# A GLA and ConvFFN layer: row squares from row tiles in the head, and three edits at the seam to the up-projection

## The chip, the cores and the metric

The kernel runs on one core of a Trainium2 chip. The metric is the device time of one execution in microseconds (us). TensorE (PE) does the matrix products, VectorE (DVE), ScalarE (ACT) and GpSimd (POOL) the elementwise work, and SyncE (SP) issues most transfers; POOL issues some.

## The reference

One layer (DEPTH is 1) of a decoder trunk, for 1024 tokens of width 1024, all in float32:

```python
x = x + gla_mixer(rms_norm(x, norm1), ...)   # 4 heads, dk 128, dv 256, chunked linear attention
x = x + conv_ffn(rms_norm(x, norm2), ...)    # below, FFN_DIM 2816
return rms_norm(x, final_norm)

def conv_ffn(x, w_up, conv_w, conv_b, w_down):
    u = x @ w_up
    u_pad = jnp.pad(u, ((0, 0), (CONV_WIDTH - 1, 0), (0, 0)))
    u = sum(u_pad[:, j:j + s] * conv_w[j] for j in range(CONV_WIDTH)) + conv_b
    gate, up = jnp.split(u, 2, axis=-1)
    return (jax.nn.silu(gate) * up) @ w_down
```

`rms_norm` multiplies each token's row by `rsqrt(mean(x*x) + 1e-6)` and a gain.

## The kernel before

**Number format.** Every operand of a product is split into two parts: a high part (a cast to the matrix format `F32R`, by ACT) and a low part, the difference (by DVE). `mm3` and `prod` add up three products: high by high, high by low, low by high. `unit(i)` loads a weight block of 128 x 1024 floats (512 KB) into a `raw` tile, of which there are four (`RAW`), and splits it into `whi` and `wlo`. For the blocks in `POOL_SPLIT` the low part is POOL's work; of these the kernel calls `unit` for four, the two plain feature tiles' gate and up weights.

**The head** (0 to about 54 us). The input comes transposed, as eight tiles `xT[kt]` of 128 features by 1024 tokens. Each is multiplied by the norm's gain and split into the big tile `T`; TensorE multiplies it with the q and k weights of head 0 (`q_ps`, `k_ps`), in a loop over `kt`. The norm's scale, one number per token, is applied behind the products. For it ACT squares each xT tile (`sq`), and POOL (the last two: DVE) adds the squares to `sqsum`; eight small products with a column of ones sum over the features (`st_ps`, line 281), giving `ss_1`, and `rsqrt` on POOL makes `rstd_1` of it. `va_mm(tok)` multiplies a tile of 128 tokens with the V weights of head 0; three of these run, then a product of `diag` (the scales on a diagonal, made by DVE) spreads the scales over the partitions (`b_ps`, `rstd_bc`), then `va_mm(3)`. In this stage the order on PE, ACT and DVE is partly as written (`manual_schedule`) and partly a scheduler's; SP's queue runs in order, and a load waits there for its buffer.

**The middle** (54 to about 420 us): linear attention by heads, the gate products, the output projection.

**The seam** (about 420 to 510 us). While the second half of the output projection runs over eight token tiles, `norm2` normalizes each and `feat` transposes it (`t_ps`, in PSUM) into `T`. For tokens 4 to 7 `combine` makes sums and differences of the four quarters of the features and tokens: POOL adds high and low parts back together (`r11`, `r21`), DVE forms `t1` and `t2` from these and from the transposes in PSUM, then the new `r11` and `r21`; all are split into `T` and `T2`, and `r21` goes to memory (`f4_dram`) and comes back as `t4`. The up-projection of the feature tiles 0 and 1 is done plainly (`plain_mm`): first with the first half of the tokens, between the last two `feat`, then with the second half, in PSUM banks that `feat`'s transposes leave. From feature tile 2 on, fewer products are formed with those sums (`xb`, `zb`, `yb`), and POOL adds up the weights (`w_prep`: `s12`, `s34`).

`plain_evac` copies the products to SBUF tiles `y` (four buffers, which the later `yg` and `yu` share); `plain_end` runs the convolution of width 3 along the tokens (`conv`: one ACT instruction, two DVE passes) in tiles `cv` (three buffers), and `gate` does Silu, the product, and the differences that the down-projection uses. From tile 2 on, the convolutions accumulate in PSUM (`ca`); the two plain ones do so in `cv`, in SBUF.

**The rest** (to the end): the up-projection to feature tile 21, the down-projection, the last norm.

Of the kernel before, what the change touches and what calls it, by code (L numbers as in the profile page):

```python
# [14 lines left out]
P = 128  # L15
# [17 lines left out]
RAW = 4  # L33
Y_POOL = (1, 3, 5)
Y_DVE = (6,)
SQ_HP = 5
Q1_A = 2
Q1_B = 3
HALF = 512
# [4 lines left out]
U_O = U_R + 8  # L44
U_F = U_O + 8
N_UNITS = U_F + 3 * NF

POOL_SPLIT = {U_F, U_F + 1, U_F + 2, U_F + 3, U_F + 4, U_F + 5}

V_N1 = 0  # L50
V_BA = V_N1 + KT
# [6 lines left out]
def gla_convffn_kernel(  # L58
# [22 lines left out]
    def load_unit(i):  # L81
        raw = wp.tile([P, 1024], F32, name="raw", tag="raw", bufs=RAW)
        nc.sync.dma_start(out=raw, in_=w[i])
        return raw

    def split_unit(raw, eng):
        hi = wp.tile([P, 1024], F32R, name="whi", tag="whi", bufs=5)
        lo = wp.tile([P, 1024], F32R, name="wlo", tag="wlo", bufs=5)
        nc.scalar.copy(out=hi, in_=raw)  # L89
        eng.tensor_tensor(out=lo, in0=raw, in1=hi.bitcast(F32), op=ALU.subtract)  # L90
        return hi, lo

    def unit(i):
        return split_unit(load_unit(i), nc.gpsimd if i in POOL_SPLIT else nc.vector)

    def mm3(outs, ah, al, bh, bl, start, stop):
        n = len(outs)
# [56 lines left out]
    ast = g1.tile([P, S], F32R, name="ast")  # L154
    ust = g1.tile([P, 4 * P], F32R, name="ust")

    sqsum = g1.tile([P, S], F32, name="sqsum", tag="tmp1")

    def tmp2():
        return g1.tile([P, S], F32, name="tmp2", tag="tmp2")  # L160

# [5 lines left out]
    for kt in range(KT):  # L167
# [35 lines left out]
        if kt == 1:  # L203
            for j in range(2):
                nc.scalar.copy(out=wh[j][:, 256:], in_=wr[j][:, 256:])
                nc.vector.tensor_tensor(out=wl[j][:, 256:], in0=wr[j][:, 256:],
                                        in1=wh[j][:, 256:].bitcast(F32), op=ALU.subtract)
        with tc.high_priority() if kt >= SQ_HP else nullcontext():
            if kt == 0:
                nc.scalar.activation(out=sqsum, in_=raw, func=AF.Square)  # L210
            else:
                sq = g1.tile([P, S], F32, name="sq", tag="tmp2" if kt % 2 else "q_f")
                nc.scalar.activation(out=sq, in_=raw, func=AF.Square)
                eng = nc.gpsimd if kt < KT - 2 else nc.vector
                eng.tensor_tensor(out=sqsum, in0=sqsum, in1=sq, op=ALU.add)
        for ps, whi, wlo in ((q_ps, wh[0], wl[0]), (k_ps, wh[1], wl[1])):
            ks = slice(kt * P, kt * P + P)
            for ns in ([[0], [1]] if kt == 0 else [[0, 1]]):
# [57 lines left out]
    ss_1 = const.tile([P, NG], F32, name="ss_1")  # L276
    ET = mybir.EngineType
    with tc.manual_schedule(engines={ET.PE, ET.Activation, ET.DVE}):
        st_ps = sm.tile([P, NG], F32, name="st_ps", tag="sm")
        for j in range(NG):  # L280
            nc.tensor.matmul(out=st_ps[:, j:j + 1], lhsT=sqsum[:, j * P:(j + 1) * P], rhs=ones[:, 0:1],
                             start=True, stop=True)
        nc.scalar.copy(out=ss_1, in_=st_ps)
        rsqrt(rstd_1, ss_1, D)
        va_ps = [va_mm(tok) for tok in range(3)]
        rhl = [const.tile([P, NG], F32R, name=f"rhl{i}") for i in range(2)]
        nc.vector.tensor_copy(out=rhl[0], in_=rstd_1)
        nc.vector.tensor_tensor(out=rhl[1], in0=rstd_1, in1=rhl[0].bitcast(F32), op=ALU.subtract)
        diag = [g1.tile([P, S], F32R, name=f"diag{i}", tag=f"tmp{i + 1}") for i in range(2)]
        va_evac(0, va_ps[0])  # L290
        for dg, r in zip(diag, rhl):
            nc.vector.tensor_tensor(out=dg.rearrange("p (j t) -> p j t", t=P),
                                    in0=ident.unsqueeze(1).broadcast_to([P, NG, P]),
                                    in1=r.bitcast(F32).unsqueeze(2).broadcast_to([P, NG, P]), op=ALU.mult)
        for n in range(2):
            b_ps = sm.tile([P, HALF], F32, name="b_ps", tag="sm")
            for i in range(2):
                nc.tensor.matmul(out=b_ps, lhsT=ones_r, rhs=diag[i][:, n * HALF:(n + 1) * HALF],
                                 start=i == 0, stop=i == 1)
            nc.scalar.copy(out=rstd_bc[:, n * HALF:(n + 1) * HALF], in_=b_ps)  # L300
            if n == 0:
                va_evac(1, va_ps[1])
        va_ps.append(va_mm(3))
        q_f, k_f = evac_qk(q_ps, k_ps)
# [302 lines left out]
    def combine(t, tb):  # L607
        cs = slice(t * P, (t + 1) * P)
        b12, b22 = tb
        r11, r21, t1, t2 = (rp.tile([P, 4, P], F32, name=n, tag=n) for n in ("r11", "r21", "t1", "t2"))  # L610
        pool_add(r11, T[:, 4, :, cs].bitcast(F32), T[:, 5, :, cs].bitcast(F32))
        pool_add(r21, T[:, 6, :, cs].bitcast(F32), T[:, 7, :, cs].bitcast(F32))
        nc.vector.tensor_tensor(out=t1, in0=r11, in1=b12, op=ALU.subtract)
# [85 lines left out]
    def cv_tile(name):  # L699
        return up.tile([P, S], F32, name=name, tag="cv", bufs=3)  # L700
# [43 lines left out]
        return ys  # L744

    def plain_end(f, ys):
        c = [conv(f, j, ys[j]) for j in range(2)]
        gate(f, c[0], c[1], c[0])

    def w_load(f):  # L750
        return [load_unit(U_F + 3 * f + j) for j in range(2)] if f < NF else None
# [42 lines left out]
            down_mm(bx[t], g, t, i == 0, i == NP2 - 1)  # L794

    with tc.manual_schedule(engines={ET.PE}):
        plain_end(0, plain_evac(0))
        y_last = plain_evac(NPLAIN - 1)

        def finish_products(st):  # L800
            f, xb, zb, wf, yg, yu = st
# [20 lines left out]
        pB_stack.close()  # L822
        pC_stack = ExitStack()
        pC = pC_stack.enter_context(tc.tile_pool(name="pC", bufs=1, space=PSUM, reuse_waits="tile"))
        prev, wn = None, w_load(NPLAIN)
        for f in range(NPLAIN, NF + 1):
            p4, q3 = finish_products(prev) if prev else (
                lambda: None, lambda: plain_end(NPLAIN - 1, y_last))
            if f == NF:
                break  # L830
            if f == NP2:
# [275 lines left out]
```

## Time and profile before

| what | value |
| --- | --- |
| device time, median of 3 runs | 1091.33 us (1090.83 to 1092.58) |
| the profiled execution's own time | 1091.58 us |
| its span in the profile | 1089.8 us |
| TensorE busy | 1068.9 us, 98% |
| DVE, ACT, POOL busy | 730.6, 507.7, 328.9 us |
| mean granted TensorE clock | 0.992 |
| moved by DMA | 149.07 MB, mean 137 GB/s |

The span reaches from the first to the last recorded instruction; the execution's own time is 1.78 us longer. Busy times are of single engines, and overlap. The granted clock is a share of 2.4 GHz: 1.00 is that, 0.50 is 1.2 GHz.

### The profile page before, as it was taken

The page shows a single profiled execution, that of the slowest core. Times are in us where ns is not written, and L with a number is a line of the kernel's source. Part 1 is how long each engine was busy: PE and PEld are TensorE (multiplying, and loading weights), DVE is VectorE, ACT ScalarE, POOL GpSimd, SP SyncE. Part 2 cuts the span into 40 slices and gives each one's busy share as a digit, 9 for nine tenths or more (in the row PEclk, how much of TensorE's full clock was granted, in tenths as well). Part 3 has the DMA queues.
Part 4 walks back from the last instruction along what each step waited for, and adds up shares of the span by engine and source line. Part 5 has one row for each costly group of instructions (what it writes and reads, how often), then busy time and mean ns, then how long its engine had stood idle before and what let it go on. Part 6 is the DMA issues. An engine that isn't in the chain of part 4 may idle for free.

```text
span 1089.8 us, 14045 instructions
## 1 busy us (share of the span) xinstructions
PE 1068.9 (98%) x5288; PEld 905.3 (83%) x5288; DVE 730.6 (67%) x888; ACT 507.7 (47%) x779; POOL 328.9 (30%) x273
## 2 busy tenths in 40 slices
PE   7999999999999999898999999999999999999997
PEld 5889999898888888787888888888888888888885
DVE  7757767575534146867767677677767767997863
ACT  6444636364323035364545455445444545544453
POOL 5100100030631022537443423554645431200311
PEclk8999999999999999999999999999999999999999
DMA  5511111140523131135343434544554469976472
GB/s 203 184 40 59 58 68 50 67 174 32 190 81 126 49 106 39 39 122 197 135 156 116 155 127 155 153 106 126 159 140 108 126 169 329 379 245 198 157 258 90
DMA packets 62996, 149.07 MB, mean 137 GB/s; under 512 B 7120, under 2 KB 9936, under 8 KB 62416
## 3 DMA queue, kind: packets, MB, share of 16 engines
q1 hardware_dynamic: 54240, 125.89, 33.8%
q0 software_dynamic: 8688, 22.29, 8.6%
q8 instruction: 41, 0.67, 0.2%
q14 instruction: 27, 0.22, 0.1%
HBM read 102.80 MB, written 45.35 MB: 136 GB/s over the span
## 4 chain that ended last, share of the span: by engine, by line
PE 91%; DVE 3%; DMA 2%; POOL 2%; ACT 1%; issue 1%; SPq 0%; POOLq 0%; ACTq 0%; DVEq 0%
PE xb L574 20%; PE zb L574 10%; PE bw L776 8%; PE bx L776 5%; PE yb L574 5%; PE o_ps L99 3%; PE o_ps L103 3%; PE o_ps L101 3%; PE bz L776 3%; PE by L776 3%; PE r_ps L99 3%; PE r_ps L103 3%; PE r_ps L101 3%; PE v_ps L103 2%; PE v_ps L99 2%; PE v_ps L101 2%
## 5 line engine op out<-in xcount | busy, mean ns | idle before, releaser
L574 PE MATMUL xb<-T,whi 128*128 128x512 f32 x640 | 198.4, 391 | 3.0 <-ACT yg L841 3.0
L574 PEld LDWEIGHTS xb<-T,whi 128*128 128x128 f32 x640 | 120.8, 189 | 28.5 <-ACT yg L841 3.4
L574 PE MATMUL xb<-T,wlo 128*128 128x512 f32 x320 | 125.0, 391 | 0.0
L548 DVE TENSOR_TENSOR wlo<-s,whi 128x1024 fp32r<-128x1024 f32 x40 | 67.2, 1680 | 54.0 <-ACT whi L547 54.0
L566 POOL TENSOR_TENSOR s<-raw 128x512 f32<-128x512 f32 x40 | 60.4, 1512 | 128.2 <-DVE wlo L548 83.4
L574 PE MATMUL zb<-T,whi 128*128 128x512 f32 x320 | 98.5, 389 | 0.0
L574 PEld LDWEIGHTS xb<-T,wlo 128*128 128x128 f32 x320 | 60.5, 189 | 12.6
L574 PEld LDWEIGHTS zb<-T,whi 128*128 128x128 f32 x320 | 60.1, 188 | 12.5
L566 POOL TENSOR_TENSOR cv<-cv 128x512 f32<-128x512 f32 x14 | 33.2, 2371 | 113.7 <-DVE cv L722 108.4
L481 POOL DMA_DIRECT2D o_dram<-o_sb x16 | 12.0, 749 | 178.1 <-DVE o_sb L476 121.4
L566 POOL TENSOR_TENSOR s<-s,raw 128x512 f32<-128x512 f32 x40 | 64.3, 1607 | 1.6
L548 DVE TENSOR_TENSOR wlo<-raw,whi 128x1024 fp32r<-128x1024 f32 (+1 forms) x40 | 42.2, 1054 | 33.3 <-ACT whi L547 33.3
L574 PE MATMUL zb<-T,wlo 128*128 128x512 f32 x160 | 62.2, 389 | 0.0
L89 ACT CAST whi<-raw 128x1024 fp32r<-128x1024 f32 x32 | 33.6, 1051 | 51.4 <-PE o_ps L103 34.3
L547 ACT CAST whi<-s 128x1024 fp32r<-128x1024 f32 x40 | 42.0, 1050 | 32.6 <-PE xb L574 25.9
L547 ACT CAST whi<-raw 128x1024 fp32r<-128x1024 f32 (+1 forms) x40 | 33.3, 834 | 47.6 <-PE zb L574 29.8
L99 PE MATMUL v_ps<-whi,T 128*128 128x256 f32 x192 | 54.5, 284 | 0.0
L103 PE MATMUL v_ps<-whi,T 128*128 128x256 f32 x192 | 54.5, 284 | 0.0
L101 PE MATMUL v_ps<-wlo,T 128*128 128x256 f32 x192 | 54.4, 283 | 0.0
L776 PE MATMUL bw<-whi 128*128 128x512 f32 x132 | 51.5, 390 | 0.0
L776 PE MATMUL bw<-whi,wlo 128*128 128x512 f32 x132 | 51.4, 389 | 0.0
L776 PE MATMUL bw<-wlo,whi 128*128 128x512 f32 x132 | 51.3, 389 | 0.0
(291 smaller groups left out, 2971.3 us busy)
## 6 DMA issues: line engine op xcount, KB each, us to landing
raw<-in_w_dram SPq DMA_DIRECT2D x74, 512.0 KB, 3.6
t_dram<-cv SPq DMA_DIRECT2D x44, 256.0 KB, 2.6
t_dram<-cv POOLq DMA_DIRECT2D x33, 256.0 KB, 6.7
t<-in_w_dram SPq DMA_DIRECT2D x33, 256.0 KB, 4.0
t<-t_dram SPq DMA_DIRECT2D x33, 256.0 KB, 4.2
ab<-in_w_dram SPq DMA_DIRECT2D x32, 256.0 KB, 3.5
h_dram<-cv SPq DMA_DIRECT2D x14, 512.0 KB, 4.2
ab<-h_dram SPq DMA_DIRECT2D x21, 256.0 KB, 3.0
```

The source lines that it names most:

```text
L89: nc.scalar.copy(out=hi, in_=raw)
L99: nc.tensor.matmul(out=outs[j], lhsT=ah, rhs=bh[j], start=start, stop=False)
L101: nc.tensor.matmul(out=outs[j], lhsT=ah, rhs=bl[j], start=False, stop=False)
L103: nc.tensor.matmul(out=outs[j], lhsT=al, rhs=bh[j], start=False, stop=stop)
L481: nc.gpsimd.dma_start(out=o_dram[:, g - 1:g + 1, h * DV:(h + 1) * DV], in_=o_sb)
L547: nc.scalar.copy(out=dst_hi, in_=src)
L548: nc.vector.tensor_tensor(out=dst_lo, in0=src, in1=dst_hi.bitcast(F32), op=ALU.subtract)
L566: nc.gpsimd.tensor_tensor(out=out, in0=a, in1=b, op=op)
L574: nc.tensor.matmul(out=out, lhsT=a[:, ks], rhs=b[:, kt, :], start=start and kt == 0 and j == 0, stop=kt == 3 and j == 2, skip_group_check= ...
L776: nc.tensor.matmul(out=out, lhsT=a[:, ts], rhs=b[:, H1], start=start and j == 0, stop=stop and j == 2, skip_group_check=True)
```

## The change

1. In the head the squares of the xT tiles and `st_ps` go. Instead SP loads the input a second time, as eight tiles `xr` of 128 tokens by 1024 features (`xt`), and ACT squares each with the row sum (`accum_out`) going straight to a column of `ss_1`.
2. `POOL_SPLIT` goes: the low parts of the four plain weight blocks are DVE's.
3. `r11` and `r21` of `combine` get two buffers each.
4. All plain products are evacuated first. The plain convolutions run behind the closing of `pB`, in PSUM tiles of `pC` that share the tag `c0`; the up half comes first, its second pass goes to a `cv` tile, and the gated product to a tile `h`.

```diff
--- before.py
+++ after.py
@@ -33,7 +33,6 @@
 RAW = 4
 Y_POOL = (1, 3, 5)
 Y_DVE = (6,)
-SQ_HP = 5
 Q1_A = 2
 Q1_B = 3
 HALF = 512
@@ -44,8 +43,6 @@
 U_O = U_R + 8
 U_F = U_O + 8
 N_UNITS = U_F + 3 * NF
-
-POOL_SPLIT = {U_F, U_F + 1, U_F + 2, U_F + 3, U_F + 4, U_F + 5}
 
 V_N1 = 0
 V_BA = V_N1 + KT
@@ -91,7 +88,7 @@
         return hi, lo
 
     def unit(i):
-        return split_unit(load_unit(i), nc.gpsimd if i in POOL_SPLIT else nc.vector)
+        return split_unit(load_unit(i), nc.vector)
 
     def mm3(outs, ah, al, bh, bl, start, stop):
         n = len(outs)
@@ -153,8 +150,6 @@
     rstd_bc = g1.tile([P, S], F32, name="rstd_bc")
     ast = g1.tile([P, S], F32R, name="ast")
     ust = g1.tile([P, 4 * P], F32R, name="ust")
-
-    sqsum = g1.tile([P, S], F32, name="sqsum", tag="tmp1")
 
     def tmp2():
         return g1.tile([P, S], F32, name="tmp2", tag="tmp2")
@@ -205,14 +200,6 @@
                 nc.scalar.copy(out=wh[j][:, 256:], in_=wr[j][:, 256:])
                 nc.vector.tensor_tensor(out=wl[j][:, 256:], in0=wr[j][:, 256:],
                                         in1=wh[j][:, 256:].bitcast(F32), op=ALU.subtract)
-        with tc.high_priority() if kt >= SQ_HP else nullcontext():
-            if kt == 0:
-                nc.scalar.activation(out=sqsum, in_=raw, func=AF.Square)
-            else:
-                sq = g1.tile([P, S], F32, name="sq", tag="tmp2" if kt % 2 else "q_f")
-                nc.scalar.activation(out=sq, in_=raw, func=AF.Square)
-                eng = nc.gpsimd if kt < KT - 2 else nc.vector
-                eng.tensor_tensor(out=sqsum, in0=sqsum, in1=sq, op=ALU.add)
         for ps, whi, wlo in ((q_ps, wh[0], wl[0]), (k_ps, wh[1], wl[1])):
             ks = slice(kt * P, kt * P + P)
             for ns in ([[0], [1]] if kt == 0 else [[0, 1]]):
@@ -276,11 +263,10 @@
     ss_1 = const.tile([P, NG], F32, name="ss_1")
     ET = mybir.EngineType
     with tc.manual_schedule(engines={ET.PE, ET.Activation, ET.DVE}):
-        st_ps = sm.tile([P, NG], F32, name="st_ps", tag="sm")
         for j in range(NG):
-            nc.tensor.matmul(out=st_ps[:, j:j + 1], lhsT=sqsum[:, j * P:(j + 1) * P], rhs=ones[:, 0:1],
-                             start=True, stop=True)
-        nc.scalar.copy(out=ss_1, in_=st_ps)
+            xr = g1.tile([P, D], F32, name="xr", tag=("tmp1", "tmp2", "q_f", "k_f")[j % 4])
+            nc.sync.dma_start(out=xr, in_=xt[j * P:(j + 1) * P, :])
+            nc.scalar.activation(out=xr, in_=xr, func=AF.Square, accum_out=ss_1[:, j:j + 1])
         rsqrt(rstd_1, ss_1, D)
         va_ps = [va_mm(tok) for tok in range(3)]
         rhl = [const.tile([P, NG], F32R, name=f"rhl{i}") for i in range(2)]
@@ -607,7 +593,8 @@
     def combine(t, tb):
         cs = slice(t * P, (t + 1) * P)
         b12, b22 = tb
-        r11, r21, t1, t2 = (rp.tile([P, 4, P], F32, name=n, tag=n) for n in ("r11", "r21", "t1", "t2"))
+        r11, r21, t1, t2 = (rp.tile([P, 4, P], F32, name=n, tag=n, bufs=2 if n[0] == "r" else 1)
+                            for n in ("r11", "r21", "t1", "t2"))
         pool_add(r11, T[:, 4, :, cs].bitcast(F32), T[:, 5, :, cs].bitcast(F32))
         pool_add(r21, T[:, 6, :, cs].bitcast(F32), T[:, 7, :, cs].bitcast(F32))
         nc.vector.tensor_tensor(out=t1, in0=r11, in1=b12, op=ALU.subtract)
@@ -744,8 +731,8 @@
         return ys
 
     def plain_end(f, ys):
-        c = [conv(f, j, ys[j]) for j in range(2)]
-        gate(f, c[0], c[1], c[0])
+        cu = conv(f, 1, ys[1], pC.tile([P, S], F32, name="ca", tag="c0"))
+        gate(f, conv(f, 0, ys[0], pC.tile([P, S], F32, name="ca", tag="c0")), cu, cv_tile("h"))
 
     def w_load(f):
         return [load_unit(U_F + 3 * f + j) for j in range(2)] if f < NF else None
@@ -794,8 +781,7 @@
             down_mm(bx[t], g, t, i == 0, i == NP2 - 1)
 
     with tc.manual_schedule(engines={ET.PE}):
-        plain_end(0, plain_evac(0))
-        y_last = plain_evac(NPLAIN - 1)
+        ys = [plain_evac(f) for f in range(NPLAIN)]
 
         def finish_products(st):
             f, xb, zb, wf, yg, yu = st
@@ -822,10 +808,12 @@
         pB_stack.close()
         pC_stack = ExitStack()
         pC = pC_stack.enter_context(tc.tile_pool(name="pC", bufs=1, space=PSUM, reuse_waits="tile"))
+        if NPLAIN > 1:
+            plain_end(0, ys[0])
         prev, wn = None, w_load(NPLAIN)
         for f in range(NPLAIN, NF + 1):
             p4, q3 = finish_products(prev) if prev else (
-                lambda: None, lambda: plain_end(NPLAIN - 1, y_last))
+                lambda: None, lambda: plain_end(NPLAIN - 1, ys[-1]))
             if f == NF:
                 break
             if f == NP2:
```

SP's queue in the head, before, from xT tile 3 on (`raw_199`; `raw_218` to `raw_275` are xT tiles 4 to 7, `raw_299` and `raw_304` the V weights):

```order
L186 DMA raw_199<-in_xT_dram 128x1024
L223 DMA ident_69<-in_cst_dram 128x128
L225 DMA war_295<-in_wa_dram 128x128
L240 DMA vec_sb_68<-in_vec_dram 128x188
L241 DMA mask_70<-in_cst_dram 128x128
L186 DMA raw_218<-in_xT_dram 128x1024
L186 DMA raw_237<-in_xT_dram 128x1024
L186 DMA raw_256<-in_xT_dram 128x1024
L186 DMA raw_275<-in_xT_dram 128x1024
L83 DMA raw_299<-in_w_dram 128x1024
L83 DMA raw_304<-in_w_dram 128x1024
```

The same place now, from the third row tile on (two more `xr` stand right ahead; `raw_207`, `raw_223`, `raw_239` and `raw_255` are xT tiles 4 to 7, `raw_276` and `raw_281` the V weights):

```order
L268 DMA xr_298<-in_xt_dram 128x1024
L181 DMA raw_207<-in_xT_dram 128x1024
L181 DMA raw_223<-in_xT_dram 128x1024
L181 DMA raw_239<-in_xT_dram 128x1024
L268 DMA xr_301<-in_xt_dram 128x1024
L181 DMA raw_255<-in_xT_dram 128x1024
L268 DMA xr_304<-in_xt_dram 128x1024
L268 DMA xr_307<-in_xt_dram 128x1024
L268 DMA xr_310<-in_xt_dram 128x1024
L80 DMA raw_276<-in_w_dram 128x1024
L80 DMA raw_281<-in_w_dram 128x1024
L268 DMA xr_313<-in_xt_dram 128x1024
```

Three row tiles now stand ahead of xT tile 4, one ahead of tile 7, three ahead of the V weights and one behind them.

ACT's queue in the seam, before, around the copy of the first `yg` (`y_4401` and `y_4404` are the second plain tile's products, `xb_4437` the first sums' product):

```order
L547 CAST T_66<-t4_4360 128x1024
L547 CAST T_66<-t4_4364 128x1024
L727 ACTIVATE cv_4388<-cv_4384 128x512
L547 CAST whi_4528<-raw_4496 128x1024
L742 COPY y_4404<-u_ps_4335 128x512
L711 ACTIVATE cv_4470<-y_4404,vec_sb_68 128x1024
L841 COPY yg_4439<-xb_4437 128x512
L721 ACTIVATE cv_4466<-cv_4466 128x1024
```

And now (`y_4372` and `y_4369` are the first plain tile's, up and gate; `y_4378` the second's up):

```order
L533 CAST whi_4525<-raw_4493 128x1024
L729 COPY y_4378<-u_ps_4326 128x512
L698 ACTIVATE ca_4385<-y_4372,vec_sb_68 128x1024
L704 COPY cv_4386<-ca_4385 128x2
L829 COPY yg_4433<-xb_4431 128x512
L698 ACTIVATE ca_4391<-y_4369,vec_sb_68 128x1024
L533 CAST whi_4533<-s12_4529 128x1024
L834 COPY yg_4433<-xb_4431 128x512
```

Ahead of the copy of `yg` there was the second plain tile's last convolution; now the first plain tile's first one stands there, with its two-column copy.

DVE's queue in the seam, before, from the first plain convolution on:

```order
L712 SCALAR_TENSOR_TENSOR cv_4384<-y_4378,vec_sb_68,cv_4384 128x1023
L548 TENSOR_TENSOR wlo_4416<-raw_4411,whi_4415 128x1024
L714 SCALAR_TENSOR_TENSOR cv_4384<-y_4378,vec_sb_68,cv_4384 128x1022
L712 SCALAR_TENSOR_TENSOR cv_4388<-y_4381,vec_sb_68,cv_4388 128x1023
L548 TENSOR_TENSOR wlo_4424<-s12_4419,whi_4423 128x1024
L714 SCALAR_TENSOR_TENSOR cv_4388<-y_4381,vec_sb_68,cv_4388 128x1022
L548 TENSOR_TENSOR wlo_4430<-s34_4420,whi_4429 128x1024
L548 TENSOR_TENSOR wlo_4434<-raw_4413,whi_4433 128x512
L722 TENSOR_TENSOR cv_4384<-cv_4384,cv_4388 128x1024
L712 SCALAR_TENSOR_TENSOR cv_4466<-y_4401,vec_sb_68,cv_4466 128x1023
L548 TENSOR_TENSOR T_66<-t4_4360,T_66 128x1024
```

And now, from the first weight split of the up-projection on:

```order
L534 TENSOR_TENSOR wlo_4410<-raw_4405,whi_4409 128x1024
L534 TENSOR_TENSOR wlo_4418<-s12_4413,whi_4417 128x1024
L534 TENSOR_TENSOR wlo_4424<-s34_4414,whi_4423 128x1024
L534 TENSOR_TENSOR wlo_4428<-raw_4407,whi_4427 128x512
L534 TENSOR_TENSOR T_66<-t4_4351,T_66 128x1024
L534 TENSOR_TENSOR T_66<-t4_4355,T_66 128x1024
L534 TENSOR_TENSOR wlo_4526<-raw_4493,whi_4525 128x1024
L699 SCALAR_TENSOR_TENSOR ca_4385<-y_4372,vec_sb_68,ca_4385 128x1023
L701 SCALAR_TENSOR_TENSOR cv_4386<-y_4372,vec_sb_68,ca_4385 128x1022
L699 SCALAR_TENSOR_TENSOR ca_4391<-y_4369,vec_sb_68,ca_4391 128x1023
L701 SCALAR_TENSOR_TENSOR ca_4391<-y_4369,vec_sb_68,ca_4391 128x1022
```

The passes of the first plain tile stood between the splits of feature tile 2's weights; now all splits up to the first of feature tile 3 come before them.

## Rows read from the trace of the kernel before

**Rows 1.** The page, part 1: busy us, share of span, instructions of TensorE.
```profile
PE 1068.9 (98%) x5288; PEld 905.3 (83%) x5288; DVE 730.6 (67%) x888; ACT 507.7 (47%) x779; POOL 328.9 (30%) x273
```

**Rows 2.** Waits of TensorE, whole span: us in total, times, longest.
```profile
PE q_ps L101 <- DVE T L197: 5.0, 2, 3.9
PE u_ps L574 <- DVE t L614: 3.6, 1, 3.6
PE xb L574 <- ACT yg L841: 3.0, 1, 3.0
```

**Rows 3.** Timeline of the head: start us, us, engine, what; idle before, releaser.
```profile
13.80 0.73 PE L99 MATMUL q_ps<-T,whi 128*128 128x512 f32 x2
...
14.85 12.21 POOL L215 TENSOR_TENSOR sqsum<-sqsum,sq 128x1024 f32<-128x1024 f32 x4 [0.98 <-ACT sq L213]
...
18.91 1.22 PE L101 MATMUL q_ps<-T,whi 128*128 128x512 f32 x2 [3.91 <-DVE T L197]
...
32.90 0.61 PE L99 MATMUL q_ps<-T,whi 128*128 128x512 f32 x2
...
38.34 1.84 PE L281 MATMUL st_ps<-ones,sqsum 128*128 128x1 f32 x16
...
41.53 0.16 ACT L283 COPY ss<-st_ps 128x8 f32<-128x8 f32 x1
...
44.67 2.35 DVE L292 TENSOR_TENSOR diag<-ident,rhl 128x1024 fp32r<-128x1024 f32 x2
...
50.40 0.40 PE L266 MATMUL va_ps<-T 128*128 128x288 f32 x1 [0.21 <-ACT rstd_bc L300]
```

**Rows 4.** Windows of the head: busy by engine, TensorE clock, DMA share, GB/s.
```profile
0.00:9.00 9.00, 7.23 (x23) 5.72 (x24) 2.67 (x6) 4.07 (x6) 0.71 (x8) 1.00 0.65 201
9.00:12.00 3.00, 3.00 (x11) 2.36 (x11) 1.28 (x2) 2.86 (x4) 0.68 (x1) 1.00 1.03 417
12.00:15.00 3.00, 3.00 (x13) 1.92 (x11) 3.00 (x2) 3.00 (x4) 2.02 (x2) 1.00 0.88 299
36.00:39.00 3.00, 3.00 (x19) 2.57 (x17) 2.01 (x3) 1.74 (x2) 0.00 (x0) 1.00 0.97 365
```

**Rows 5.** ACT, a Square with row sum: ns min/median/max, first and last start.
```profile
L601 ACT ACTIVATE junk<-x2a x4: 1041/1044/1047, 394.1 to 411.4; 128x1024 bf16<-128x1024 f32 x4
L601 ACT ACTIVATION_READ_ACCUMULATOR junk<-x2a x4: 187/190/194, 395.0 to 412.4; 128x1 f32 x4
```

**Rows 6.** Timeline of the seam, first stall.
```profile
453.22 1.03 PE L629 MATMUL t_ps<-ident,x2b 128*128 128x128 f32 x8
...
454.61 2.69 POOL L566 TENSOR_TENSOR r<-T 128x512 f32<-128x512 f32 x2 [6.20 <-DVE T L548]
...
460.33 1.28 DVE L632 TENSOR_TENSOR T<-t_ps,T 128x512 fp32r<-128x512 f32 x2
...
463.35 0.70 PE L574 MATMUL u_ps<-T,whi 128*128 128x512 f32 x2 [3.64 <-DVE t L614]
...
474.55 1.05 ACT L547 CAST whi<-raw 128x1024 fp32r<-128x1024 f32 x1 [1.99 <-DMA raw<-in_w_dram]
```

**Rows 7.** Timeline of the seam, second stall.
```profile
489.15 4.44 POOL L566 TENSOR_TENSOR cv<-cv 128x512 f32<-128x512 f32 x1 [5.29 <-ACT T L547]
...
493.63 1.24 ACT L711 ACTIVATE cv<-y,vec_sb 128x1024 f32<-128x1024 f32 x1 [2.53 <-POOL cv L566]
...
495.39 1.22 PE L574 MATMUL xb<-T,whi 128*128 128x512 f32 x2 [2.97 <-ACT yg L841]
```

**Rows 8.** Windows behind the two stalls of the seam.
```profile
464.00:468.00 4.00, 4.00 (x13) 3.13 (x12) 2.26 (x4) 1.40 (x3) 0.00 (x0) 0.57 0.24 66
495.00:499.00 4.00, 3.61 (x9) 2.90 (x10) 4.00 (x2) 1.29 (x2) 4.00 (x3) 0.57 1.02 335
```

**Rows 9.** DVE convolution passes, on PSUM (ca) and on SBUF (cv): ns min/median/max.
```profile
L712 DVE SCALAR_TENSOR_TENSOR ca<-yu,ncw,ca x8: 1287/1289/1289, 513.0 to 646.3; 128x1023 f32<-128x1023 f32 x8
...
L712 DVE SCALAR_TENSOR_TENSOR cv<-y,vec_sb,cv x4: 1277/1286/2295, 472.6 to 496.8; 128x1023 f32<-128x1023 f32 x4
```

## The prediction

> **What bounds the kernel now.** The page's engine table comes first: TensorE is busy for 98% of the span [rows 1]. Time can then only be won where TensorE waits or runs at a lower clock, so the list of its waits is next. It has three long entries [rows 2]: 5.0 us in the head (a T low half from DVE), 3.6 us and 3.0 us in the seam. None of the others is above 1.0 us, and none lies between 54 and 450 us or behind 500 us. The change touches just these two places; of the instructions behind them only names and line numbers differ.
>
> In the head, the timeline [rows 3] shows TensorE at contraction tile 2 (13.80 us), then idle until 18.91 us, because DVE's low halves are slow while POOL adds squares (four adds, 12.21 us, from 14.85 us). The adds end in eight small products `st_ps` that keep TensorE for 1.84 us. The next landmark is `va_mm(3)`, which starts at 50.40 us.
>
> In the seam the first stall (463.35 us) is for `t2` of the last `combine` [rows 6]: its row sums on POOL waited 6.20 us for the one buffer of `r11` at 454.61 us, which slid the combine for token tile 7 behind them, while its transposes had been done at 454.25 us. The second stall (495.39 us) is for the copy of `yg` [rows 7]: ACT stood 2.53 us at a convolution whose `cv` buffer POOL still wrote (a 4.44 us subtraction) and the copy was queued behind it. Behind each stall TensorE's mean granted clock is 0.57 over four us [rows 8], a mix of 1.2 and 2.4 GHz.
>
> **The head, step by step.** Removed: the squares of the xT tiles, POOL's and DVE's adds and `st_ps`. Added: eight loads of 0.524 MB on SP's queue, three of them in front of xT tile 4, and eight Squares of 1.04 + 0.19 = 1.24 us on ACT [rows 5]. POOL's adds no longer disturb DVE, so tiles 2 and 3 run through. What is late next is the transfer of xT tile 4. I do that as a ledger.
>
> The rate: three stretches with a full queue moved 417, 299 and 365 GB/s at DMA shares of 1.03, 0.88 and 0.97 [rows 4]; rate over share is 405, 340 and 376, and I take 375, their mean (the bounds are 299 and 417). At 9.0 us 201 x 9 = 1.81 MB had moved [rows 4] of the 3.44 MB issued up to `mask`. Tile 4 ends after 1.63 + three row tiles + itself = 3.73 MB, which is 9.95 us: 18.95 us, and 19.35 us with 0.4 us to signal it (an estimate of mine). Its cast takes about 1.1 us (like the Square of that size) and its low half 1.28 us (like DVE's instruction of that size, [rows 9]).
>
> TensorE takes 2.72 us per tile (two from 32.90 to 38.34 us, [rows 3]), so from 13.80 us it wants tile 4 at 19.24 us and gets the high half at 20.45: a wait of 1.2 us, and 0.4 us more for the low half, since only four products (0.9 us) can run ahead of it. The later tiles land every 1.4 us and are in time. The loop ends at 13.80 + 6 x 2.72 + 1.6 = 31.7 us.
>
> The first V weights are eight transfers behind tile 4: 18.95 + 8 x 1.40 + 0.4 = 30.55 us, split by 32.9 us, another wait of 1.0 us. From the end of `st_ps` to `va_mm(3)` it was 50.40 - 40.18 = 10.2 us; with the wait that gives 42.9 us, and I add 0.6 us because `rstd_bc`'s copy now stands behind more weight casts on ACT: 43.5 us. The last row tile lands at 33.35 us; its Square ends at 34.6; from `ss_1` to the end of `diag` it took 5.3 us (41.69 to 47.02 us, [rows 3]), and one weight split of 1.28 us stands in between: 41.2 us, just ahead of the 41.6 us at which TensorE asks for it. So the head gives 50.4 - 43.5 = **6.9 us**. The same ledger with 299 GB/s brings `va_mm(3)` to 50.5 us (nothing won), with 417 to 41.7 us (8.7 us). A lower clock after a wait is not in the sum: 1.6 us is half of the shortest wait that a drop followed here (2.97 us, [rows 7]).
>
> The Trainium skill speaks against part of this: "DMA: Bandwidth & Descriptors", section Where 436 GB/s comes from, puts the limit of a core's HBM-to-SBUF transfers near 358 GB/s. The trace does not agree, with 417 GB/s over three us and 365 over another three [rows 4]; by the page the ledger would give 44.8 us and the head 5.6 us, so the sum would end 1.3 us higher.
>
> **The seam, step by step.** The four weight splits go from POOL to DVE, where they cost 1.2 to 1.3 us each (as [rows 9]) at places where DVE waits for TensorE anyway; POOL then has nothing in front of the row sums, and with two buffers they run before their transposes. For token tile 7: transposes at 454.25 us, a cast of 0.5, two low halves 1.28 us [rows 6], then `t1` and `t2`, which with the release took from 461.61 to 463.35 us, 1.74 us: the bank is free at 457.8 us, 1.9 us before TensorE comes at 459.71 us (463.35 - 3.64). The first stall goes: 3.64 us and its clock, 4 x (1 - 0.57) = 1.72 us [rows 8].
>
> The first weights of the up-projection were ready 14.2 us after those low halves began (460.33 to 474.55 us, [rows 6]); now they are ready at 454.8 + 14.2 = 469.0 us. The 96 products of the second half end at 459.71 + 21.8 = 481.5 us, `xb` and `zb` at 486.95 us, and then TensorE needs the copy of `yg`. On ACT that copy follows the last `y` evacuation, the scaled input of the first convolution (1.2 us) and the two-column copy; that one waits for DVE's two passes (2 x 1.28 us, [rows 9]). From 481.5 us: casts and evacuation to 482.7, input 483.9, the passes 484.1 to 486.7, two columns 486.9, `yg` 487.5 us. A wait of 0.6 us replaces 2.97 + 1.72 us. That DVE passes on PSUM hold 1.28 us whatever POOL does, while those on SBUF reach 2.3 us, is in [rows 9]. The second pair of convolutions slides into the next iteration, where DVE gets 4 x 1.28 us more in front of `yg += zb`; I allow 0.9 us there (bounds 0 and 2.6, two passes). Sum: 10.05 - 1.5 = **8.5 us** (5.4 to 10).
>
> **Sum.** The profiled execution took 1091.58 us, 1.78 more than its span and 0.25 more than the median. 1091.6 - 6.9 - 8.5 = **1076.2 us**.
>
> **The rivals.**
> *The head gives nothing.* The transfers run at the 299 GB/s of one row; TensorE waits 3.7 us at tile 4 and again at V. 1091.6 - 8.5 = 1083.1 us. For it: between 9 and 35 us the queue never empties now. Against it: 365 and 417 GB/s in the other rows. Chance 0.15.
> *The second stall stays.* The copy of `yg` still stands behind a convolution; if the weights land 2 to 3 us later than I reckon, the wait is back at 3 us with its clock. The seam gives 5.4 us, the total is 1079.3 us. For it: all of the margin is the 0.6 us above. Against it: the loads are released by `r21`, which is no longer late. Chance 0.13.
> *Slower.* In the head every xT tile queues behind row tiles. If the queue keeps only the 201 GB/s of its first 9 us [rows 4], tile 4 comes 8 us late and `rstd_1` later still; `va_mm(3)` starts near 68 us, 17.7 us late, and the total is 1100.8 us. It decides below some 245 GB/s, where the head loses what the seam gives. Against it: in those 9 us the queue was still filling. Chance 0.05.
> *No change.* The time won comes back as waits further on. No row behind 500 us shows TensorE near a wait, so 0.04, at 1091 us.
> The forecast has the remaining 0.63.
>
> **How the numbers follow.** The forecast's own range, from the bounds, is 1073 to 1080 us. Down to 1071.5 and up to 1084 us it takes in the first two rivals. A measurement of this kernel tells about 0.2% (2.2 us) from no change. Faster: 0.63 + 0.15 + 0.13 = 0.91; same 0.04; slower 0.05.
>
> **What will show it.** Head: no wait at tile 2, one of 1 to 2 us at tile 4 released by DMA through a cast, `va_mm(3)` near 43 us. Seam: no wait of TensorE on `t`, and one below a us on `yg`; clock 1.00 from 440 us on. I am wrong if the granted clock drops in the head after the tile 4 wait, if `diag` comes later than the third `va_ps`, or if TensorE waits for `yg += zb` for more than 2 us in the up-projection's second iteration.

## The result and the profile after

The changed kernel takes 1074.56 us (median, 1074.11 to 1075.29) against 1091.26 us: a ratio of 0.9846, 95% interval 0.9829 to 0.9863, or 16.8 us. A second set gave 0.9826 (0.9807 to 0.9844). The forecast was 1076.2 us, in a range of its own of 1073 to 1080 us, and of 1071.5 to 1084 us with its first two rivals. The profiled execution took 1075.29 us, with a span of 1073.5.

The page of the changed kernel, busy us of the engines, which answers to [rows 1]:

```profile
PE 1062.3 (99%) x5272; PEld 900.1 (84%) x5272; DVE 709.8 (66%) x890; ACT 509.4 (47%) x788; POOL 293.5 (27%) x264
```

The list of TensorE's waits in the changed kernel, which answers to [rows 2]: us in total, times, longest.

```profile
PE w_ps L159 <- POOL ones L111: 1.0, 1, 1.0
PE q_ps L96 <- DVE whi L195: 0.7, 1, 0.7
PE va_ps L253 <- ACT rstd_bc L286: 0.6, 1, 0.6
PE xb L560 <- ACT yg L829: 0.4, 1, 0.4
PE k_ps L96 <- DVE whi L195: 0.4, 1, 0.4
PE va_ps L254 <- DVE wlo L225: 0.4, 1, 0.4
PE q_ps L96 <- ACT T L191: 0.3, 1, 0.3
```

The three long entries of before are gone, and none above 1.0 us has come in their place. In a second profile of the changed kernel the wait at xT tile 4 is 1.2 us, the others again at most 1.0. Line numbers are 3 to 14 lower than before.

The timeline of the head after, which answers to [rows 3]:

```profile
18.53 1.06 ACT L269 ACTIVATE xr<-xr 128x1024 f32<-128x1024 f32 x1 [0.17 <-DMA xr<-in_xt_dram]
...
19.76 3.71 ACT L191 ACTIVATE T<-raw,n_sb 128x1024 fp32r<-128x1024 f32 x3
...
20.97 0.73 PE L96 MATMUL q_ps<-T,whi 128*128 128x512 f32 x2 [0.34 <-ACT T L191]
...
33.08 0.39 PE L254 MATMUL va_ps<-wlo,T 128*128 128x256 f32 x1 [0.35 <-DVE wlo L225]
...
34.30 0.19 ACT L269 ACTIVATION_READ_ACCUMULATOR xr<-xr 128x1 f32 x1
...
42.01 1.10 PE L284 MATMUL b_ps<-diag,ones_r 128*128 128x512 f32 x4
43.72 0.40 PE L253 MATMUL va_ps<-T 128*128 128x288 f32 x1 [0.62 <-ACT rstd_bc L286]
```

The high half of xT tile 4 (L191) is cast right behind the Square of the third row tile, the last Square ends at 34.5 us, and TensorE does not wait for `diag` at 42.01 us. `va_mm(3)` starts at 43.72 us instead of 50.40.

Windows of the head after, columns as in [rows 4]:

```profile
0.00:9.00 9.00, 6.98 (x22) 5.52 (x23) 2.67 (x6) 3.12 (x5) 0.71 (x8) 1.00 0.66 209
9.00:12.00 3.00, 3.00 (x8) 2.34 (x7) 1.58 (x2) 2.68 (x3) 0.00 (x0) 1.00 1.02 409
12.00:15.00 3.00, 3.00 (x12) 2.40 (x11) 2.77 (x4) 2.33 (x4) 0.00 (x0) 1.00 1.06 383
...
27.00:30.00 3.00, 3.00 (x15) 2.49 (x14) 0.35 (x1) 2.04 (x5) 0.00 (x0) 1.00 1.03 406
```

From 9 us on POOL is idle in these windows, and the queue moves 383 to 409 GB/s.

The head's stall had a lower clock behind it too, which the prediction does not name. The same window before and after, clock third from the right:

```profile
18.00:24.00 6.00, 5.09 (x12) 4.03 (x13) 6.00 (x4) 4.00 (x4) 5.92 (x2) 0.50 0.21 65
```

```profile
18.00:24.00 6.00, 5.53 (x23) 3.95 (x22) 3.05 (x3) 5.31 (x8) 0.00 (x0) 1.00 1.03 412
```

The groups of the Squares of the row tiles after, which answer to [rows 5], ns min/median/max:

```profile
L269 ACT ACTIVATE xr<-xr x8: 1060/1062/1065, 15.9 to 33.3; 128x1024 f32<-128x1024 f32 x8
L269 ACT ACTIVATION_READ_ACCUMULATOR xr<-xr x8: 183/185/187, 16.9 to 34.3; 128x1 f32 x8
```

The timeline of the seam after, which answers to [rows 6, 7]:

```profile
442.74 2.66 POOL L552 TENSOR_TENSOR r<-T 128x512 f32<-128x512 f32 x2 [4.77 <-DVE T L534]
...
446.48 1.03 PE L616 MATMUL t_ps<-ident,x2b 128*128 128x128 f32 x8
...
450.08 0.68 DVE L601 SCALAR_TENSOR_TENSOR t<-t,t_ps 128x512 f32<-128x512 f32 x1
...
461.96 1.05 ACT L533 CAST whi<-raw 128x1024 fp32r<-128x1024 f32 x1 [2.92 <-DMA raw<-in_w_dram]
...
480.61 0.74 PE L560 MATMUL xb<-T,whi 128*128 128x512 f32 x2 [0.44 <-ACT yg L829]
```

POOL's row sums run 3.7 us ahead of the last `feat`'s transposes, and `t2` ends 4.3 us behind the start of these (10.0 us before). The transposes come 6.74 us earlier than before (453.22), which is what the head gave; the rest of the span's 16.3 us, 9.6 us, is the seam's.

Windows of the seam after, which answer to [rows 8] (clock in the third column from the right), and the passes on PSUM of the plain convolutions, which answer to [rows 9]:

```profile
448.00:452.00 4.00, 4.00 (x19) 3.29 (x19) 4.00 (x8) 1.44 (x4) 0.00 (x0) 1.00 0.23 66
...
480.00:484.00 4.00, 3.56 (x16) 2.82 (x16) 2.26 (x2) 2.18 (x4) 1.79 (x2) 1.00 0.26 75
```

```profile
L699 DVE SCALAR_TENSOR_TENSOR ca<-y,vec_sb,ca x4: 1277/1288/1290, 477.2 to 494.6; 128x1023 f32<-128x1023 f32 x4
```

### The profile page after: what moved, and what is told of

The parts are those of the page before. It is cut to its first block, busy times and chain, and to the rows that moved or that the text cites. A ratio compares the mean times of both kernels' runs of the same rounds, so it can differ in the third digit from the quotient of the medians.

```text
span 1073.5 us, 14018 instructions
## 1 busy us (share of the span) xinstructions
PE 1062.3 (99%) x5272; PEld 900.1 (84%) x5272; DVE 709.8 (66%) x890; ACT 509.4 (47%) x788; POOL 293.5 (27%) x264
## 4 chain that ended last, share of the span: by engine, by line
PE 95%; DMA 3%; ACT 1%; DVE 1%; SPq 0%; issue 0%; POOLq 0%; POOL 0%; ACTq 0%
PE xb L560 20%; PE zb L560 10%; PE bw L763 8%; PE bx L763 6%; PE yb L560 5%; PE u_ps L560 4%; PE o_ps L96 3%; PE o_ps L100 3%; PE o_ps L98 3%; PE bz L763 3%; PE by L763 3%; PE r_ps L96 3%; PE r_ps L100 3%; PE r_ps L98 3%; PE v_ps L100 2%; PE v_ps L96 2%
## 5 line engine op out<-in xcount | busy, mean ns | idle before, releaser
L552 POOL TENSOR_TENSOR s<-raw 128x512 f32<-128x512 f32 x40 | 56.9, 1426 | 139.1 <-DVE wlo L534 87.0
L552 POOL TENSOR_TENSOR s<-s,raw 128x512 f32<-128x512 f32 x40 | 61.5, 1538 | 1.6
L86 ACT CAST whi<-raw 128x1024 fp32r<-128x1024 f32 x32 | 33.6, 1051 | 50.5 <-PE o_ps L100 34.3
L552 POOL TENSOR_TENSOR cv<-cv 128x512 f32<-128x512 f32 x12 | 26.5, 2209 | 108.5 <-DVE cv L709 108.5
```

The lines of the kernel that those rows point to most:

```text
L552: nc.gpsimd.tensor_tensor(out=out, in0=a, in1=b, op=op)
```

## Experiments

The kernel before scattered from 1090.6 to 1096.5 us over the sets, so ratios against its runs of the same set are given, with 95% intervals; us in brackets are the gain, one minus the ratio, times 1091.3 us.

### Do head and seam add up?

Edit 1 alone, in the kernel before:

```
-                eng = nc.gpsimd if kt < KT - 2 else nc.vector
-                eng.tensor_tensor(out=sqsum, in0=sqsum, in1=sq, op=ALU.add)
...
+            nc.sync.dma_start(out=xr, in_=xt[j * P:(j + 1) * P, :])
+            nc.scalar.activation(out=xr, in_=xr, func=AF.Square, accum_out=ss_1[:, j:j + 1])
```

> The kernel before with edit 1 alone (row squares from row tiles in the head). Theory: head and seam are independent, so this gives what the trace after showed at the landmark of the seam (feat(7)'s transposes 6.74 us earlier): 1091.3 - 6.7 = 1084.6 us, with both seam stalls (3.6 and 3.0 us) still in the list of TensorE's waits. Rival A: the two places help each other, and the head alone gives less, because TensorE then waits longer for weights in the seam: 1087 us or more, with a seam stall above 4 us. Rival B: the head gives nothing by itself: 1091 us.

Ratio 0.9947, 0.9932 to 0.9962 (5.8 us). TensorE's waits with edit 1 alone:

```profile
PE xb L563 <- ACT yg L830: 3.7, 1, 3.7
PE u_ps L563 <- DVE t L602: 3.3, 1, 3.3
PE q_ps L99 <- ACT T L194: 1.2, 1, 1.2
```

Both seam stalls are there, the first 0.3 us shorter and the second 0.7 us longer. The theory's 6.7 us are inside the interval (4.1 to 7.4 us). Edits 2 to 4 alone:

```
-        return split_unit(load_unit(i), nc.gpsimd if i in POOL_SPLIT else nc.vector)
+        return split_unit(load_unit(i), nc.vector)
...
+        r11, r21, t1, t2 = (rp.tile([P, 4, P], F32, name=n, tag=n, bufs=2 if n[0] == "r" else 1)
...
+        cu = conv(f, 1, ys[1], pC.tile([P, S], F32, name="ca", tag="c0"))
```

> The kernel before with edits 2 to 4 alone (the seam). Theory: what is left of the gain, 16.7 - 6.7 = 10.0 us: 1081.3 us, both seam stalls gone and the 3.9 us wait at tile 2 of the head still there. Rival: by the terms of the prediction, 8.5 us: 1082.8 us. Rival of interaction: the seam alone gives 12 us or more or 6 us or less, so that the two parts don't add up.

Ratio 0.9905, 0.9890 to 0.9920 (10.4 us); the longest waits left are 3.9 us at tile 2 of the head and 1.0 us at the start. The product of the two ratios, 0.9853, is inside the interval of all edits together: if the two places act on each other, it is by less than the 2 us or so that these runs can tell.

### Is it POOL that held DVE in the head?

Five POOL additions put back into the changed kernel:

```
+    nc.gpsimd.memset(rstd_bc, 0.0)
...
+        if 1 <= kt <= 5:
+            rv = rstd_bc.rearrange("p (h t) -> p h t", h=2)
+            nc.gpsimd.tensor_tensor(out=rv, in0=rv, in1=T[:, i_hi:i_hi + 5:4, kt % 4, :].bitcast(F32), op=ALU.add)
```

> The changed kernel with five additions of 128x1024 on POOL put back into the head; each adds the high half of an xT tile to a buffer that nothing else uses yet, so that no engine waits for their result until rstd_bc is written. What the kernel computes stays the same. Theory: what held TensorE at tile 2 of the head before was DVE's low halves, slow while POOL adds. Then DVE's low halves of tiles 2 to 5 go from 1.28 to about 2.3 us, TensorE waits about 3 us at tiles 2 to 4 again, with some clock behind it: 1074.6 + 3 to 6 = 1078 to 1081 us. Rival: the gain came from the removed products and from ACT's order; POOL's additions cost nothing: 1074.6 us within 1 us, and low halves of 1.28 us.

Ratio 0.9895, 0.9881 to 0.9910: 1080.43 us, 5.9 us above the changed kernel (5.3 us by the ratios). That this is near the 5.8 us of edit 1 is luck: `st_ps` is not back, and the stall is longer than before. TensorE's longest wait, at tile 2:

```profile
PE q_ps L98 <- DVE T L194: 6.3, 1, 6.3
```

DVE's groups in the head of the changed kernel, busy us and mean ns:

```profile
L192 DVE SCALAR_TENSOR_TENSOR T<-raw,n_sb,T 128x1024 fp32r<-128x1024 f32 x7 | 9.0, 1285 | 7.7 <-ACT T L191 7.7
...
L218 DVE TENSOR_TENSOR T<-war,T 128x128 fp32r<-128x128 f32 x1 | 0.3, 289 | 0.0
```

The same groups with POOL's additions, which take 2.99 us each:

```profile
L194 DVE SCALAR_TENSOR_TENSOR T<-raw,n_sb,T 128x1024 fp32r<-128x1024 f32 x7 | 13.0, 1888 | 2.6 <-ACT T L193 2.6
...
L223 DVE TENSOR_TENSOR T<-war,T 128x128 fp32r<-128x128 f32 x1 | 2.5, 2476 | 0.0
```

No engine waits for these sums in that stretch, so the theory holds: POOL's instructions cost through DVE's. It had put about 3 us at tiles 2 to 4; the one wait is longer because the two weight splits in front of tile 2's low half took 6.18 us together (1.82 in the changed kernel), and that low half 3.37 us. The small subtraction says how: 128x128 grows by 2.19 us. It is not slowed by a factor of its own; it runs from 24.21 to 26.69 us, and POOL's last addition from 23.3 to 26.54 us, so it looks like a wait for most of that addition. "SBUF — State Buffer" of the Trainium skill, section SBUF: two separate sides, says that a DVE instruction with two SBUF inputs and a GpSimd one that reads SBUF lock their common port pair for a whole instruction instead of sharing it; the row agrees.

### What do the row tiles' transfers cost?

Row tiles held back until xT tile 4 is cast:

```
+            nc.gpsimd.tensor_copy(out=xr[:, 0:1], in_=T[:, hid(0, 4, 0), 0, 0:1].bitcast(F32))
             nc.sync.dma_start(out=xr, in_=xt[j * P:(j + 1) * P, :])
```

> The changed kernel with each row tile's load held back until xT tile 4 has been cast (a one-element copy on POOL into the row tile in front of its load), so that xT tiles 4 to 7 are transferred ahead of all row tiles. Theory: the row tiles ahead of xT tile 4 are what makes it late; its wait (0.34 us, and 0.3 us more for the low half) goes, V weights and row tiles come no later than now: 1074.6 - 0.5 = 1074.1 us, within 1 us of the changed kernel. Rival: the transfers moved behind now make the last row tile late; diag comes after the third va_ps, and TensorE waits 1 to 4 us there: 1076 to 1079 us.

Ratio 0.9891, 0.9873 to 0.9909: 1080.58 us, 6 us above the changed kernel. The loop over the xT tiles does run through (the first `va_ps` at 29.96 us, 32.44 in the changed kernel), but V1 and two further weights are loaded ahead of the last four row tiles; the last Square ends at 41.3 us. In the timeline and the window behind it:

```profile
45.85 0.76 PE L285 MATMUL b_ps<-diag,ones_r 128*128 128x512 f32 x1 [4.79 <-DVE diag L279]
```

```profile
45.00:48.00 3.00, 1.86 (x4) 1.20 (x5) 2.24 (x3) 0.56 (x2) 0.00 (x0) 0.50 0.00 0
```

The rival was right, with a larger price: `diag` comes 4.8 us after TensorE asks for it, and the clock is at 1.2 GHz behind the wait. Early xT tiles were worth nothing here, since the row sums became late. A written order between the two, SP in the order of the program:

```
+    sp_order.enter_context(tc.manual_schedule(engines={mybir.EngineType.SP}))
...
+            if kt >= 4:
+                xr_load()
...
+        for i in range(2 * j + 1):
+            xr_load()
+    sp_order.close()
```

> The changed kernel with SP's loads of the head in a written order: ident, war, vec_sb and mask, then xT tile 4, row tile 0, xT tile 5, row tile 1, and so on to xT tile 7 and row tile 3, then V0, row tile 4, V1, and the last three row tiles. In the run with late row tiles xT tile 4 was cast at 15.98 us; at 1.29 us for each transfer after it (0.524 MB at the 405 GB/s of the changed kernel's head) xT tile 7 lands at 23.7 us, V0 at 26.2, V1 at 28.8, the last row tile at 34.0 us. Theory: the loop over the xT tiles runs through and ends near 30.0 us (32.4 us in the changed kernel), diag comes 6.6 us behind the last Square at 35.5 us or a little earlier, TensorE waits 0.5 to 1.5 us for it, and va_mm(3) starts near 42 us, 1.5 to 2 us earlier than in the changed kernel: 1072.8 us. Rival: the wait for diag is above 2 us and the granted clock drops behind it: 1075 to 1077 us, no better than the changed kernel.

Ratio 0.9858, 0.9844 to 0.9871 (1076.91 us): the rival again, no better than the changed kernel's 0.9846, whose interval overlaps. A weight load slipped in ahead of the last row tile, the last Square ended at 36.4 us, and TensorE waited 2.4 us for `diag` in two pieces. With row tile 4 in `rstd_bc`, a fifth buffer, no weight slips in:

```
+        xr = rstd_bc if j == 4 else g1.tile([P, D], F32, name="xr", tag=("tmp1", "tmp2", "q_f", "k_f")[(j - (j > 4)) % 4])
```

> The changed kernel with the loads in the written order (row tiles between xT tiles) and a fifth buffer for row tiles (rstd_bc, which nothing needs until the scales are spread), so that no weight load slips in front of the last row tile. Theory: the last Square ends 1.3 us earlier than in the run with four buffers (36.4 us), diag with it, TensorE waits 0.5 to 1 us for diag instead of 2.4 us, no lower clock follows, and va_mm(3) starts at about 42.3 us instead of 43.7: 1.0 to 1.5 us faster than the changed kernel. Rival: V1's low half, asked for at 31.7 us, and diag still make TensorE wait 2 us in all, with a lower clock behind it: no faster than the changed kernel or up to 2 us slower.

> The changed kernel once more, as the measure for the three others of this set: ratio to the kernel before 0.985.

Ratio 0.9825, 0.9806 to 0.9845, against 0.9826 of the changed kernel in the same set (1074.30 and 1074.70 us; 0.985 was expected of the latter): no difference that can be measured. In the timeline the last Square ends at 34.6 us and TensorE waits for `diag` in two pieces, and for the scales:

```profile
40.12 0.47 PE L302 MATMUL b_ps<-diag,ones_r 128*128 128x512 f32 x1 [0.59 <-DVE diag L296]
41.16 0.97 PE L302 MATMUL b_ps<-diag,ones_r 128*128 128x512 f32 x3 [0.57 <-DVE diag L296]
42.64 0.40 PE L274 MATMUL va_ps<-T 128*128 128x288 f32 x1 [0.51 <-ACT rstd_bc L304]
```

TensorE asks for `diag` at 40.12 - 0.59 = 39.5 us, and at 41.61 in the changed kernel of that set; but `va_mm(3)` starts at 42.64 and 42.92 us. Of the 2.1 us won in front, 1.8 are lost again, most of them in these three waits: in these three runs, with the queue full from 9 to 36 us, the order of its loads mostly chose where TensorE waits. No version beat the changed kernel.

### Which edit removes which seam stall?

Each of the edits 2, 3 and 4 alone, in the kernel before. Edit 3:

```
+        r11, r21, t1, t2 = (rp.tile([P, 4, P], F32, name=n, tag=n, bufs=2 if n[0] == "r" else 1)
```

> The kernel before with edit 3 alone (two buffers each for r11 and r21). Theory: the 6.2 us for which POOL's row sums waited for the buffer is what made the last combine late, so two buffers alone remove the first seam stall with its clock (3.6 + 1.7 = 5.3 us), and the second one stays near 3.0 us with its clock: 1091.3 - 5.3 = 1086.0 us. Rival A: without edit 2 POOL's three weight splits (8.6 us from 433 us on) still stand in front of the sums and DVE is late anyway; the first stall stays at 2 us or more: 1089 us. Rival B: the time won in the first stall comes back in the second (6 us instead of 3): 1090 us.

Ratio 0.9983, 0.9974 to 0.9992 (1.9 us). The first stall is gone, and the second has grown, as rival B said; waits and timeline of edit 3 alone:

```profile
PE xb L574 <- ACT yg L842: 5.7, 1, 5.7
```

```profile
486.78 4.44 POOL L566 TENSOR_TENSOR cv<-cv 128x512 f32<-128x512 f32 x1 [5.29 <-ACT T L547]
...
493.01 1.22 PE L574 MATMUL xb<-T,whi 128*128 128x512 f32 x2 [5.69 <-ACT yg L842]
```

TensorE asks for the copy of `yg` at 493.01 - 5.69 = 487.3 us, 5.1 us earlier than before (495.39 - 2.97 = 492.4, [rows 7]); POOL's subtraction in front of it starts only 2.4 us earlier (489.15). So 2.7 us of the time won are waited for again. Edit 2:

```
-        return split_unit(load_unit(i), nc.gpsimd if i in POOL_SPLIT else nc.vector)
+        return split_unit(load_unit(i), nc.vector)
```

> The kernel before with edit 2 alone (the four low parts on DVE, single buffers kept). DVE's order around the last two combines changes with it. Theory: the single buffer is the cause, so TensorE still waits 2 us or more for t, POOL's sums still wait for the release of the buffer, and the time is 1089.5 to 1091.3 us. Rival: POOL's splits were the cause, by DVE's slow instructions while they run (a 128x512 pass of 2.89 us at 439 us); then the first stall goes with single buffers too: 1086.0 us.

Ratio 0.9975, 0.9964 to 0.9985 (2.7 us). By the ratio that is 1088.6 us, just under the theory's range, and the theory was wrong: with single buffers too the wait for `t` is gone, and the second stall is again 5.7 us. The timeline shows why, at the last pass of an earlier `combine`, before and with edit 2 alone:

```profile
439.28 2.89 DVE L616 SCALAR_TENSOR_TENSOR r<-t,r 128x512 f32<-128x512 f32 x1
```

```profile
435.63 0.69 DVE L616 SCALAR_TENSOR_TENSOR r<-t,r 128x512 f32<-128x512 f32 x1
...
455.56 2.68 POOL L566 TENSOR_TENSOR r<-T 128x512 f32<-128x512 f32 x2 [3.21 <-DVE T L548]
```

Beside POOL's splits the pass took 2.89 us instead of 0.69, and ended at 442.17 us instead of 436.32. With single buffers the delay is handed on: POOL's next sums wait for `r21`'s transfer to memory and start at 444.96 us instead of 439.12, DVE waits for POOL's sums (1.76 and 1.41 us before), POOL again for DVE, and POOL's last sums start at 460.49 us instead of 455.56. DVE's order changes a little with the edit too; how much of the lead is from that was not tried. Edit 4:

```
-        plain_end(0, plain_evac(0))
-        y_last = plain_evac(NPLAIN - 1)
+        ys = [plain_evac(f) for f in range(NPLAIN)]
...
+        plain_end(0, ys[0])
```

> The kernel before with edit 4 alone (plain convolutions behind the closing of pB, in PSUM). Theory: the second seam stall (2.97 us and 1.7 us of clock) becomes a wait of about 0.5 us for the copy of yg, the first stall stays at 3.6 us: 1091.3 - 4.2 = 1087.1 us. Rival: that wait hangs on the weights, which are late while the first stall is there; the second stall stays above 2 us: 1090 to 1091 us. The sum test: if edits 2 to 4 act apart, the gains of this run, of edit 2 alone and of edit 3 alone add up to the 10 to 11 us of the seam.

Ratio 0.9956, 0.9943 to 0.9970 (4.8 us). The gain is near the theory's 4.2 us, but not by its path: the second stall shrinks to 1.8 us and not to 0.5, since the weights are still late (the first is cast 15.5 us before TensorE asks for the copy of `yg`, 18.2 us before in the changed kernel). The first stays. Its timeline, and two windows, behind the first stall and around the second:

```profile
464.58 0.70 PE L574 MATMUL u_ps<-T,whi 128*128 128x512 f32 x2 [3.65 <-DVE t L614]
...
493.82 0.73 PE L574 MATMUL xb<-T,whi 128*128 128x512 f32 x2 [1.76 <-ACT yg L841]
```

```profile
464.00:468.00 4.00, 3.42 (x15) 2.86 (x16) 3.50 (x6) 2.10 (x4) 0.36 (x1) 1.00 0.12 35
...
492.00:496.00 4.00, 2.24 (x10) 1.80 (x10) 2.12 (x2) 1.76 (x3) 3.65 (x3) 1.00 0.27 109
```

Then the changed kernel without edit 3, and without edit 2 (the diffs above, reversed):

> The changed kernel without edit 3 (single buffers for r11 and r21). The runs of single edits showed that edit 2 alone and edit 3 alone each remove the first seam stall. Theory: either is enough, so this is as fast as the changed kernel within 0.7 us, with no wait for t and one of 0.4 to 1 us for the copy of yg. Rival: with single buffers the weights come a few us later, and the wait for the copy of yg grows to 2 us or more: 2 to 4 us slower than the changed kernel.

Ratio 0.9837, 0.9818 to 0.9857 (1075.64 us, 0.9 above the changed kernel of the set), with a wait of 1.5 us for `yg`.

> The changed kernel without edit 2 (POOL makes the four low parts). Theory: as for the run without edit 3, the same time as the changed kernel within 0.7 us. Rival: DVE's passes of 2.9 us while POOL splits make the combine late, and the wait for t or for yg is back: 2 to 4 us slower.

Ratio 0.9842, 0.9823 to 0.9862 (1076.29 us, 1.6 above). TensorE's longest wait without edit 2:

```profile
PE xb L561 <- ACT yg L830: 1.7, 1, 1.7
```

Neither run has a wait for `t`. Both lie 0.2 to 0.9 us above what the theory allowed, and the longer wait for `yg` (1.5 and 1.7 instead of 0.4 us) is of that size; the differences themselves are inside what these runs can tell, since the intervals overlap.

So edits 2 and 3 are alternatives for the first stall. Alone each is worth little, because TensorE then reaches the second stall sooner; edit 4 turns the time won into time saved. The sum test comes out near (1.9 + 2.7 + 4.8 = 9.4 us against 10.4), but this is luck and does not show that the three act apart: edits 2 and 3 remove the same stall, and beside edit 4 either of them alone is enough. Edit 4 moves the plain convolutions into PSUM and behind the evacuations at once; what each of the two is worth, and what edits 2 and 3 give together without it, was not tested.

## Why the prediction was right

**Where time can be won.** Right: the three long waits were the prize, and but for `st_ps` (1.7 us) the gain is theirs and their clock's.

**Head, mechanism.** Right, by the run with POOL's additions put back. **Head, size.** 6.9 us forecast; 6.74 us at the seam's landmark, 5.8 us (4.1 to 7.4) for edit 1 alone. That the two agree so well is in part luck, as two errors met in it. The rate was not 375 GB/s but 383 to 409. The ledger also let transfers end one after another; but several are under way at once, and bytes of later ones are in its sum. By 15 us 209 x 9 + 3 x (409 + 383) = 4.26 MB had moved, and the third row tile (5.01 MB in the ledger) should at 400 GB/s have been there at 16.9 us; its Square waits for it until 18.53 us. So tile 4's cast starts at 19.76 us instead of 19.35. Its products start at 20.97 us in the changed kernel's profile and at 20.78 us with edit 1 alone, for a forecast of 20.45; the wait ahead of them is 0.3 and 1.2 us (forecast 1.2), as TensorE was later or earlier at tile 2 (15.02 us in the changed kernel's profile, 13.80 before). The 0.4 us for signalling are shown by no run by themselves. V waits 0.35 us instead of 1.0, since the loop ends at 32.4 us instead of 31.7. The waits of `va_mm(3)` for the scales (0.62 us) and `diag` (not late at 42.01 us) came as forecast, and how thin that margin is the three runs on the order of the loads show.

From tile 2 to the end of the loop TensorE took 24.5 us before (13.80 to 38.34) and 17.4 us now (15.02 to 32.44). Of these 7.1 us some 2.6 are the lower clock (an estimate: half of the 5.3 us from 18.91 to 24.20 us, which ran at 0.50); the rest is the two waits of before (5.0 us) less what TensorE now waits at tile 4. `st_ps` adds 1.7 us; 1.2 us are lost ahead of tile 2 and 0.9 us behind the loop.

Some prices at other rates do not follow from the ledger's steps. Redone, these give `va_mm(3)` at about 49 us with 299 GB/s (50.5 is written) and about 64 us with 201 GB/s (68 is written), and the head loses what the seam gives below some 225 GB/s instead of 245. The full queue of the changed kernel was never near these rates.

"DMA: Bandwidth & Descriptors" of the Trainium skill, section Where 436 GB/s comes from, gives about 358 GB/s for this path; 383 to 409 GB/s over the windows above do not agree, and the head did not lose the 1.3 us that this would have cost.

**Seam.** 8.5 us forecast; 9.6 us by the spans, 10.4 us (8.7 to 12.0) by edits 2 to 4 alone. The bank is free at 450.76 + 6.74 = 457.5 us (forecast 457.8), the weights are cast at 468.7 (469.0), the wait for `yg` is 0.44 us (0.6), and DVE's passes on PSUM hold 1.28 us. The mis-sized term is the 0.9 us allowed for `yg += zb`: TensorE doesn't wait there. Without it, 10.05 - 0.44 = 9.6 us. That sum counts 1.72 us of lower clock behind each stall, as the profile before had it; other executions have another price (last section).

**A rival's price.** "The second stall stays" was put at 5.4 us for the seam. Edits 2 and 3, each alone, come nearest to that case: 1.9 and 2.7 us. I took the stalls as separate; but what ends the second moves by less than half of what TensorE gains (2.4 of 5.1 us with edit 3), and the rest is waited for there.

**The other rivals.** The head's transfers never fell to 299 or 201 GB/s while the queue was full. "No change", a ratio of 1, lies outside the interval (0.9829 to 0.9863). Slower did not happen, but the run with late row tiles shows its mechanism, `rstd_1` too late, at 6 us.

## What to carry to other kernels

When two stalls stand in a row on the same engine, removing the first may only lengthen the second: look whether what ends the second moves with the first, and change both before judging either. Work on POOL while it would be idle is not free: look in the trace for DVE instructions of one form with two durations. With a full queue, reordering loads moved the wait here instead of removing it, so the load that feeds the longest chain (here row tile to `diag`) must not slip back.

## What was not expected of the hardware

The granted clock does not follow from the length of a wait. After 3.64 us it was 0.57 over four us [rows 8]; after 3.65 us at the same place, with edit 4 alone, it was 1.00. After waits of 1.85 and 0.57 us with one product between them, in the written order with four buffers, it fell: windows of that run, clock third from the right,

```profile
42.00:45.00 3.00, 2.43 (x8) 1.83 (x9) 1.63 (x3) 1.87 (x4) 0.89 (x1) 0.68 0.44 157
45.00:48.00 3.00, 3.00 (x20) 3.00 (x20) 2.17 (x3) 1.39 (x3) 0.07 (x1) 0.75 0.39 93
```

while 1.76 us (edit 4 alone, 492 us) left it at 1.00. In the head, tile 4's wait of 1.94 us with edit 4 alone was followed by 0.65 from 28 to 32 us, and one of 1.92 us with edit 3 alone by 1.00. The prediction's 1.72 us of clock behind each seam stall is therefore a price of some executions. Its margin of 1.6 us was not broken in these profiles, but the 2.97 us that it is half of are not the shortest wait with a drop behind it. What decides it was not tested.
